# A decoder trunk on one core: key and content-query projections regrouped, mask and maximum in one operation, the keys' norm scale moved to the latents

## The chip, the cores and the metric

The kernel runs on one core of a Trainium2 chip. The metric is the device time of one execution in microseconds (us). A core has a matmul engine (TensorE, PE in the profile, with PEld for its weight loads), a vector engine (DVE), an activation engine (ACT), GpSimd (POOL) and SyncE (SP), which issues DMAs. Each engine takes its instructions in the order in which they stand in its queue, and waits on semaphores for the others.

## The reference

Two layers over 256 positions of width 2048. The first mixes by a short gated convolution, the second by latent attention with 16 heads; each is followed by a squared-ReLU MLP, and every sub-layer ends in a layer norm of (alpha * x + f(x)). What matters here is the attention:

```
ckv = h @ w_dkv
c = rms_norm(ckv[..., :512], kv_norm_g)
k_pe = apply_rope(ckv[..., 512:], cos, sin)
kv = (c @ w_ukv).reshape(bsz, seq, 16, 256)      # k_nope, v: 128 + 128 a head
...
q = (rms_norm(x @ w_dq, q_norm_g) @ w_uq).reshape(bsz, seq, 16, 192)   # q_nope 128, q_pe 64
...
s = (q_nope . k_nope + q_pe . k_pe) * 192 ** -0.5
s = where(k_pos <= q_pos, s, -inf)
p = softmax(s)
o = p . v,  then o @ w_o
```

The root-mean-square norm multiplies each position by one number, so it may be taken before the up-projection (on the latents `c`) or after it (on the keys and values).

## The kernel before

Everything is in float32, and the large products keep its precision by splitting both operands into a high part that the matmul's input format holds exactly and a low remainder. A product of split operands has three parts: high by high, low weight by high data, high weight by low data. Weights stream in as 128x1024 blocks (SP's queue), ACT casts the high part (`hi`, line 139), DVE subtracts it (`lo`, line 140), and PE multiplies. At most nine pairs of such parts are held (`WA`), so a cast waits for PE to be done with the pair nine places back.

The data operand of a product holds the high part in columns 0 to 255 and the low part in columns 256 to 511 of one tile. There are two ways to multiply with it:

- `mm` (line 283, by `mm_k1`, lines 279 to 281): three matmuls of 256 columns for each 128 rows of the inner dimension, all added into one 128x256 half of a PSUM bank.
- `high` and `low` (lines 261 and 265): one matmul of 512 columns, high weight by both halves of the data, and one of 256 columns, low weight by the high half. The result lies in two halves of the bank, which `whole` (lines 405 to 407) adds up: ACT copies one half to SBUF (tile `t`), DVE adds the other.

The attention stage begins with the latents. `latent` (line 992) is called four times for the key/value side (`chl`, 4 tiles) and four times for the queries (`qhl`): it finishes the layer norm of the product (`ln.weighted`), multiplies by the norm's gain and splits (lines 996 and 997), and sums squares (1000 to 1004). `rms` (1006) makes 1/rms per position, for the keys and values as a column `rc`; PE spreads it over the partitions and ACT copies it as the row tile `rk` (1043). The gain is on the latents; the position's scale is not: keys are multiplied by `rk` when they leave PSUM (line 1083, DVE), values by `rc` (line 1106, ACT). The queries' scale is folded into the exponent (`sc`, `nsc`).

`project` (line 1074) makes one group of four heads, four times: four keys `ps_k`, two tiles of rotary queries `ps_p`, four content queries `ps_q` (line 1095, ACT copies them out), two tiles of values `ps_v`. All of them, except the values, go through `mm`, in a ring of four PSUM banks. `attend` (1109) is one head: scores into `S`, mask added (1124, DVE, 128x384: the first block of queries sees 128 keys, the second 256), maximum of each of the two blocks (1126, DVE), exponent with its sum (1129, ACT), scaling (1131 to 1133, DVE), transposes, and the product with the values. `together` (1150) starts head s, transposes for head s-2 and finishes head s-3, and the loop puts three items of the next group's `project` behind each. A tile scheduler lays the instructions of each engine in a fixed order from this; lines of the code may so stand elsewhere in a queue than the text suggests. Between them DVE and ACT also do work without haste: the splits of later weights, and `normal` (529 to 531, tile `nu`), which finishes the layer norm of the residual.

Of the kernel before, what the change touches and what calls it, by code (L numbers as in the profile page):

```python
# [10 lines left out]
F32 = mybir.dt.float32  # L11
F32R = mybir.dt.float32r
AF = mybir.ActivationFunctionType
ALU = mybir.AluOpType
AX = mybir.AxisListType

P = 128
W = 256 + 2
T = 256
# [10 lines left out]
RMS_EPS = 1e-6  # L30
SCALE = (128 + 64) ** -0.5
NEG = -1e30
LOOK = 5
RAW, WA = 7, 9
NB = 4
# [21 lines left out]
def trunk(ctx: ExitStack, tc: tile.TileContext, xT, vecs, lead, w_first, w_in, w_out, w_kv, w_q, w_uk, w_uv,  # L57
# [201 lines left out]
    def high(ps, w, blk, x, first):  # L259

        nc.tensor.matmul(ps, w[blk // 8][0][:, blk % 8, :], x, start=first, stop=False)  # L261

    def low(ps, w, blk, x, last):

        nc.tensor.matmul(ps[:, :T], w[blk // 8][1][:, blk % 8, :], x[:, :T], start=False, stop=last)  # L265
# [17 lines left out]
    def mm(ps, w, b0, xhl, nk):  # L283

        for k in range(nk):
            mm_k1(ps, w, b0 + k, xhl[k], k == 0, k == nk - 1)
# [116 lines left out]
    def whole(ps, out):  # L403

        t = tmp.tile([P, T], F32, tag="evac", name="t")
        nc.scalar.copy(t, ps[:, T:])  # L406
        nc.vector.tensor_tensor(out, ps[:, :T], t, ALU.add)  # L407
# [560 lines left out]
    with tc.tile_pool(name="att", bufs=1) as ap:  # L968
# [13 lines left out]
        def rope(src):  # L982
# [6 lines left out]
            nc.vector.tensor_tensor(a, a, b, ALU.add)  # L989
            return a  # L990

        def latent(ps, m, dst, gcol, sqs):
            f = tmp.tile([P, T], F32, tag="fh", name="lat", bufs=3)
            ln.weighted(ps, f)
            g = vec[:, gcol + m:gcol + m + 1]
            nc.scalar.activation(dst[m][:, :T], f, AF.Copy, scale=g)
            nc.vector.scalar_tensor_tensor(dst[m][:, T:], f, g, dst[m][:, :T].bitcast(F32),
                                           ALU.mult, ALU.subtract)
            if m == 0:
                nc.scalar.activation(sqs, f, AF.Square)  # L1000
            else:
                sq = tmp.tile([P, T], F32, tag="sq", name="sq")
                nc.scalar.activation(sq, f, AF.Square)
                nc.vector.tensor_tensor(sqs, sqs, sq, ALU.add)
# [31 lines left out]
        for m in range(NK):  # L1036
            ps = next(pss)
            if m == 0:
                rms(rc, csq)
            if m == 2:  # L1040
                rkp = psum("rkp")
                spread(rkp, rc)
                nc.scalar.copy(rk, rkp[:, :T])
            latent(ps, m, qhl, C_QG, qsq)
        rq = small.tile([P, 2], F32, tag="rr", name="rq")

        def query_scale():
# [15 lines left out]
        with tc.tile_pool(name="att2", bufs=2) as a2, \  # L1063
# [10 lines left out]
            def project(g, box):  # L1074

                k4, q4, v4 = (t[g % 2] for t in (k2, q2, v2))
                p4 = [p2[(2 * g + j) % 3] for j in range(2)]
                box.update(k=k4, q=q4, p=p4, v=v4)
                w = take()
                for j in range(4):  # L1080
                    ps = psum("ps_k")
                    mm(ps, w, 4 * j, chl, NK)
                    nc.vector.tensor_tensor(k4[:, j, :], ps[:, :T], rk, ALU.mult)
                    yield
                w = take(1)
                for j in range(2):
                    ps = psum("ps_p")
                    mm(ps, w, 4 * j, qhl, NK)
                    stacked(p4[j], rope(ps[:, :T]))
                    yield  # L1090
                w = take()
                for j in range(4):
                    ps = psum("ps_q")
                    mm(ps, w, 4 * j, qhl, NK)
                    nc.scalar.copy(q4[:, j, :], ps[:, :T])
                    yield
                if g == 0:
                    query_scale()
                for _ in range(4):
                    ln.normal(next(todo))  # L1100
                w = take()
                for b in range(2):
                    ps = psum("ps_v")
                    for k in range(NK):
                        dot(ps, wide_rows(w[k // 2], k % 2), held(chl[k], b), k == 0, k == NK - 1)
                    nc.scalar.activation(v4[:, b, :], ps, AF.Copy, scale=rc[:, b:b + 1])
                    yield

            def attend(h, box):

                j = h % 4
                qn, kn = box["q"][:, j, :], box["k"][:, j, :]
                qp = box["p"][j // 2][:, j % 2, :]
                S = paux.tile([P, 512], F32, tag="S", name=f"S_{h}", bufs=2)
                spans = ((0, P), (P, T))
                for b, (at, n) in enumerate(spans):
                    tok = slice(b * P, (b + 1) * P)
                    nc.tensor.matmul(S[:, at:at + n], qn[:, tok], kn[:, :n], start=True, stop=False)
                    nc.tensor.matmul(S[:, at:at + n], qp[:, tok], kph[:, :n], start=False, stop=False)
                    nc.tensor.matmul(S[:, at:at + n], qp[:, tok], kpl[:, :n], start=False, stop=True)  # L1120
                pr = pr2[h % 2]
                mx = small.tile([P, 2], F32, tag="mx", name="mx")
                su = small.tile([P, 2], F32, tag="su", name="su")
                nc.vector.tensor_tensor(pr, S[:, :3 * P], mask_t, ALU.add)
                for b, (at, n) in enumerate(spans):
                    nc.vector.tensor_reduce(mx[:, b:b + 1], pr[:, at:at + n], AX.X, ALU.max)
                nc.vector.tensor_tensor(mx, mx, nsc, ALU.mult)
                for b, (at, n) in enumerate(spans):
                    nc.scalar.activation(pr[:, at:at + n], pr[:, at:at + n], AF.Exp, bias=mx[:, b:b + 1],
                                         scale=sc[:, b:b + 1], accum_out=su[:, b:b + 1])  # L1130
                nc.vector.reciprocal(su, su)
                for b, (at, n) in enumerate(spans):
                    nc.vector.tensor_scalar(pr[:, at:at + n], pr[:, at:at + n], su[:, b:b + 1], None, ALU.mult)
                yield
                tp = paux.tile([P, 512], F32, tag="ta", name="tp")
                for n in range(3):
                    nc.tensor.transpose(tp[:, n * P:(n + 1) * P], pr[:, n * P:(n + 1) * P], id_t)
                pt = pt2[h % 2]
                nc.scalar.copy(pt, tp[:, :3 * P])
                yield  # L1140
                po = paux.tile([P, 512], F32, tag="tb", name="po")
                vv = box["v"]
                nc.tensor.matmul(po[:, :T], vv[:, 0, j * P:(j + 1) * P], pt[:, :T], start=True, stop=False)
                nc.tensor.matmul(po[:, P:T], vv[:, 1, j * P:(j + 1) * P], pt[:, T:], start=False, stop=True)
                put_split(oT[h], po[:, :T])
                yield
# [261 lines left out]
```

## Time and profile before

| | us |
|---|---|
| median of 3 runs | 1988.34 (1988.27 to 1989.27) |
| the profiled execution | 1987.44 |
| its span (first to last instruction) | 1985.7 |
| the part from the first key product to the first output product alone | 1095.6 to 1227.0 |

A timeline row gives an instruction's start (us from the span's start), its duration, engine, line and tiles. Matmuls overlap: one of 256 columns is shown with 0.28 us, yet the next starts after 0.12. So PE's cost is read as the distance of starts. The same holds, less strongly, for DVE and ACT: a 128x256 DVE operation is shown with 0.42 us and the next starts 0.34 later.

### The profile page before, as it was taken

The numbers are of one execution on the slowest core, as the hardware profiler recorded it, in microseconds if no ns is written. First come the engines' busy times: TensorE is split into PE (matmuls) and PEld (weight loads), VectorE is DVE, ScalarE is ACT, GpSimd is POOL, SyncE is SP. The second block draws the span as 40 slices with busy tenths as digits, with TensorE's granted clock in tenths as the row PEclk, the third lists the DMA queues.
The fourth block names the chain that finished last, engine by engine and source line by source line (L and its number), as shares of the span: only waits on it lengthen the run. The fifth ranks groups of instructions, "written<-read, shape, count | busy, mean of one in ns | idle before, by whom it ended". The sixth has DMA issues, their size and how long they took to land.

```text
span 1985.7 us, 29654 instructions
## 1 busy us (share of the span) xinstructions
PE 1977.9 (100%) x11048; PEld 1727.4 (87%) x11048; DVE 1748.6 (88%) x2532; ACT 1285.2 (65%) x1902; POOL 36.0 (2%) x81
## 2 busy tenths in 40 slices
PE   9999999999999999999999999999999999999998
PEld 8888888988888888888889998898888888888886
DVE  8667667786999999999898988777799999999998
ACT  7444445585767767677666766557576776767765
POOL 0000000000000000000100110000000000000010
PEclk9999999999999999999999999999999999999999
DMA  9666666573666665666865644656355666556685
GB/s 343 213 190 189 188 188 190 179 237 134 194 210 203 203 208 192 212 203 202 271 236 175 198 125 141 206 182 195 115 198 202 207 206 207 191 203 211 202 245 179
DMA packets 111840, 395.77 MB, mean 199 GB/s; under 512 B 12752, under 2 KB 14800, under 8 KB 111184
## 3 DMA queue, kind: packets, MB, share of 16 engines
q1 hardware_dynamic: 106704, 383.79, 59.2%
q0 software_dynamic: 4848, 9.96, 2.2%
q8 instruction: 86, 1.41, 0.3%
q14 instruction: 58, 0.48, 0.1%
q10 hardware_dynamic: 144, 0.13, 0.0%
HBM read 384.40 MB, written 4.19 MB: 196 GB/s over the span
## 4 chain that ended last, share of the span: by engine, by line
PE 97%; DVE 1%; ACT 1%; issue 1%; DVEq 0%; ACTq 0%
PE ps_u L261 21%; PE ps_l L261 13%; PE ps_u L265 11%; PE ps L348 8%; PE ps L349 8%; PE ps L346 8%; PE ps_l L265 7%; PE ps_d L349 2%; PE ps_d L348 2%; PE ps_d L346 2%; PE ps_w L295 1%; PE ps_w L293 1%; PE ps_w L294 1%; PE ps_g L295 1%; PE ps_g L293 1%; PE ps_g L294 1%
## 5 line engine op out<-in xcount | busy, mean ns | idle before, releaser
L140 DVE TENSOR_TENSOR lo<-raw,hi 128x1024 fp32r<-128x1024 f32 x709 | 851.3, 1221 | 115.6 <-issue 46.9
L139 ACT CAST hi<-raw 128x1024 fp32r<-128x1024 f32 x709 | 726.8, 1049 | 329.4 <-DVE raw L182 134.3
L261 PE MATMUL ps_u<-xhl,hi 128*128 128x512 f32 x1792 | 621.0, 393 | 0.1
L265 PE MATMUL ps_u<-xhl,lo 128*128 128x256 f32 x1792 | 486.1, 280 | 0.0
L261 PEld LDWEIGHTS ps_u<-xhl,hi 128*128 128x128 f32 x1792 | 329.3, 188 | 66.5 <-DVE fp L407 0.5
L265 PEld LDWEIGHTS ps_u<-xhl,lo 128*128 128x128 f32 x1792 | 338.4, 189 | 12.8
L261 PE MATMUL ps_l<-xhl_a,hi 128*128 128x512 f32 x704 | 244.1, 393 | 0.0
L265 PE MATMUL ps_l<-xhl_a,lo 128*128 128x256 f32 x704 | 195.6, 280 | 0.0
L261 PEld LDWEIGHTS ps_l<-xhl_a,hi 128*128 128x128 f32 x704 | 132.3, 188 | 29.8
L265 PEld LDWEIGHTS ps_l<-xhl_a,lo 128*128 128x128 f32 x704 | 131.9, 188 | 0.2
L177 DVE TENSOR_TENSOR raw_t<-raw,raw 128x1024 f32<-128x1024 f32 x100 | 121.9, 1219 | 0.4 <-DMA raw<-in_w2f_dram 0.4
L140 DVE TENSOR_TENSOR lo_t<-raw_t,hi_t 128x1024 fp32r<-128x1024 f32 x100 | 121.9, 1219 | 0.0
L406 ACT COPY t<-ps_u 128x256 f32<-128x256 f32 x112 | 41.4, 369 | 108.6 <-PE ps_u L265 108.4
L139 ACT CAST hi_t<-raw_t 128x1024 fp32r<-128x1024 f32 x100 | 105.2, 1052 | 0.0
L261 PE MATMUL ps_l<-z,hi 128*128 128x512 f32 x240 | 82.4, 392 | 0.0
L295 PE MATMUL ps_w<-xd,hi 128*128 128x258 f32 x256 | 72.8, 284 | 0.0
L293 PE MATMUL ps_w<-xd,hi 128*128 128x258 f32 x256 | 72.3, 283 | 0.0
L407 DVE TENSOR_TENSOR fp<-ps_u,t 128x256 f32<-128x256 f32 x112 | 47.1, 420 | 28.7 <-ACT t L406 28.5
L294 PE MATMUL ps_w<-xd,lo 128*128 128x258 f32 x256 | 72.3, 282 | 0.0
L184 DVE TENSOR_TENSOR raw<-raw 128x512 f32<-128x512 f32 x100 | 69.2, 692 | 3.5
L261 PE MATMUL ps_l<-oT,hi 128*128 128x512 f32 x208 | 71.3, 392 | 0.0
L140 DVE TENSOR_TENSOR t<-raw,t 128x512 fp32r<-128x512 f32 x100 | 68.6, 686 | 2.1 <-ACT t L139 1.0
(378 smaller groups left out, 3921.2 us busy)
## 6 DMA issues: line engine op xcount, KB each, us to landing
raw<-in_w_dram SPq DMA_DIRECT2D x312, 512.0 KB, 4.2
raw<-in_w2f_dram SPq DMA_DIRECT2D x200, 512.0 KB, 4.2
raw<-in_w_in_dram SPq DMA_DIRECT2D x88, 512.0 KB, 4.3
raw<-in_w_out_dram SPq DMA_DIRECT2D x32, 512.0 KB, 4.2
raw<-in_w_o_dram SPq DMA_DIRECT2D x32, 512.0 KB, 4.3
raw<-in_w_kv_dram SPq DMA_DIRECT2D x10, 512.0 KB, 4.8
raw<-in_w_q_dram SPq DMA_DIRECT2D x8, 512.0 KB, 4.1
raw<-in_w_uk_dram SPq DMA_DIRECT2D x8, 512.0 KB, 4.3
```

The lines of the kernel that those rows point to most:

```text
L139: nc.scalar.copy(hi, src)
L140: return nc.vector.tensor_tensor(lo, src, hi.bitcast(F32), ALU.subtract)
L177: nc.vector.tensor_tensor(t.rearrange(two, a=2), b12.unsqueeze(1).to_broadcast([P, 2, BW]), r1.rearrange(two, a=2), ALU.subtract)
L184: nc.vector.tensor_tensor(t4, b21, b12, ALU.subtract)
L261: nc.tensor.matmul(ps, w[blk // 8][0][:, blk % 8, :], x, start=first, stop=False)
L265: nc.tensor.matmul(ps[:, :T], w[blk // 8][1][:, blk % 8, :], x[:, :T], start=False, stop=last)
L293: nc.tensor.matmul(ps[:, :W], hi, x[k][:, :W], start=k == 0, stop=False)
L294: nc.tensor.matmul(ps[:, :W], lo, x[k][:, :W], start=False, stop=False)
L295: nc.tensor.matmul(ps[:, :W], hi, x[k][:, W:], start=False, stop=k == NC - 1)
L346: nc.tensor.matmul(ps, x[0], w[0], start=first, stop=False, skip_group_check=onto)
L348: nc.tensor.matmul(ps[:, at], x[0], w[1][:, at], start=False, stop=False, skip_group_check=onto)
L349: nc.tensor.matmul(ps, x[1], w[0], start=False, stop=last, skip_group_check=onto)
```

## The change

Three edits.

1. Keys and content queries use `high` and `low`, a pair for each of the four inner blocks, in place of `mm`'s three matmuls, and `whole` in place of a single operation that takes the result out of PSUM. The rotary queries keep `mm`.
2. The keys' scale goes to the latents. `latent` leaves the four key/value latents unscaled in a tile `plain`; once `rk` is there, `normed` multiplies each by `rk` and splits it. It is called for tiles 0 and 1 behind the third query latent and for 2 and 3 behind the fourth. The products by `rk` and `rc` at keys and values go; values are copied.
3. Mask and maximum are one operation for each of the two blocks, `tensor_tensor_reduce`, which writes the masked scores and the maximum.

```
@@ -989,13 +990,22 @@
+        plain = act.tile([P, NK, T], F32, tag="a1", name="plain")
+
+        def gained(dst, f, g):
+            nc.scalar.activation(dst[:, :T], f, AF.Copy, scale=g)
+            nc.vector.scalar_tensor_tensor(dst[:, T:], f, g, dst[:, :T].bitcast(F32), ALU.mult, ALU.subtract)
+
+        def normed(m):
+            f = plain[:, m, :]
+            nc.vector.tensor_tensor(f, f, rk, ALU.mult)
+            gained(chl[m], f, vec[:, C_KG + m:C_KG + m + 1])
+
         def latent(ps, m, dst, gcol, sqs):
-            f = tmp.tile([P, T], F32, tag="fh", name="lat", bufs=3)
+            f = plain[:, m, :] if dst is chl else tmp.tile([P, T], F32, tag="fh", name="lat", bufs=3)
             ln.weighted(ps, f)
-            g = vec[:, gcol + m:gcol + m + 1]
-            nc.scalar.activation(dst[m][:, :T], f, AF.Copy, scale=g)
-            nc.vector.scalar_tensor_tensor(dst[m][:, T:], f, g, dst[m][:, :T].bitcast(F32),
-                                           ALU.mult, ALU.subtract)
+            if dst is not chl:
+                gained(dst[m], f, vec[:, gcol + m:gcol + m + 1])
...
             latent(ps, m, qhl, C_QG, qsq)
+            if m >= 2:
+                for k in range(2 * m - 4, 2 * m - 2):
+                    normed(k)
...
                     ps = psum("ps_k")
-                    mm(ps, w, 4 * j, chl, NK)
-                    nc.vector.tensor_tensor(k4[:, j, :], ps[:, :T], rk, ALU.mult)
+                    for k in range(NK):
+                        high(ps, w, 4 * j + k, chl[k], k == 0)
+                        low(ps, w, 4 * j + k, chl[k], k == NK - 1)
+                    whole(ps, k4[:, j, :])
...
                     ps = psum("ps_q")
-                    mm(ps, w, 4 * j, qhl, NK)
-                    nc.scalar.copy(q4[:, j, :], ps[:, :T])
+                    for k in range(NK):
+                        high(ps, w, 4 * j + k, qhl[k], k == 0)
+                        low(ps, w, 4 * j + k, qhl[k], k == NK - 1)
+                    whole(ps, q4[:, j, :])
...
-                    nc.scalar.activation(v4[:, b, :], ps, AF.Copy, scale=rc[:, b:b + 1])
+                    nc.scalar.copy(v4[:, b, :], ps)
...
-                nc.vector.tensor_tensor(pr, S[:, :3 * P], mask_t, ALU.add)
                 for b, (at, n) in enumerate(spans):
-                    nc.vector.tensor_reduce(mx[:, b:b + 1], pr[:, at:at + n], AX.X, ALU.max)
+                    nc.vector.tensor_tensor_reduce(pr[:, at:at + n], S[:, at:at + n], mask_t[:, at:at + n], 1.0, LOW,
+                                                   ALU.add, ALU.max, mx[:, b:b + 1])
```

The scheduler lays the queues anew for this. Three places follow. In the rows, a number behind a name is that of the buffer; `ps_w` is the product for a latent, `t` an intermediate, `lat` the tile that holds `chl` and `qhl`, `kqva1` the tile of the keys and queries, `kqva2` that of values, masked scores and mask. Lines from about 1000 on stand up to 17 lines later in the changed file, those before it one line later.

**TensorE, where the last query latent ends and the first key begins**, before:

```order
L293 MATMUL ps_w_10802<-xd1_0_9688,hi353_10655 128x258
L294 MATMUL ps_w_10802<-xd1_0_9688,lo353_10656 128x258
L295 MATMUL ps_w_10802<-xd1_0_9688,hi353_10655 128x258
L279 MATMUL ps_k_10904<-lat_10352,lo354_10662 128x256
L280 MATMUL ps_k_10904<-lat_10352,hi354_10661 128x256
L281 MATMUL ps_k_10904<-lat_10352,hi354_10661 128x256
```

and with the change:

```order
L294 MATMUL ps_w_10797<-xd1_0_9688,hi353_10644 128x258
L295 MATMUL ps_w_10797<-xd1_0_9688,lo353_10645 128x258
L296 MATMUL ps_w_10797<-xd1_0_9688,hi353_10644 128x258
L262 MATMUL ps_k_10905<-lat_10352,hi354_10650 128x512
L266 MATMUL ps_k_10905<-lat_10352,lo354_10651 128x256
```

The three matmuls of an inner block are two; nothing has come between the last latent and the first key.

**DVE, from the third query latent to the first keys**, before:

```order
L542 SCALAR_TENSOR_TENSOR t_10793<-ab1_10370,wgb_10791,t_10793 128x256
L140 TENSOR_TENSOR lo359_10895<-raw359_10892,hi359_10894 128x1024
L140 TENSOR_TENSOR lo360_10901<-raw360_10898,hi360_10900 128x1024
L997 SCALAR_TENSOR_TENSOR lat_10352<-lat_10790,vec_85,lat_10352 128x256
L1004 TENSOR_TENSOR squares_10363<-squares_10363,sq_10799 128x256
L140 TENSOR_TENSOR lo361_10963<-raw361_10960,hi361_10962 128x1024
L541 TENSOR_TENSOR t_10866<-ps_w_10802,ab1_10370 128x256
L140 TENSOR_TENSOR lo362_11021<-raw362_11018,hi362_11020 128x1024
L542 SCALAR_TENSOR_TENSOR t_10866<-ab1_10370,wgb_10864,t_10866 128x256
L1083 TENSOR_TENSOR kqva1_10878<-ps_k_10904,rk_10360 128x256
L1083 TENSOR_TENSOR kqva1_10878<-ps_k_10918,rk_10360 128x256
```

and with the change:

```order
L543 SCALAR_TENSOR_TENSOR t_10782<-ab1_10371,wgb_10780,t_10782 128x256
L1001 TENSOR_TENSOR plain_10363<-plain_10363,rk_10360 128x256 x4
L997 SCALAR_TENSOR_TENSOR lat_10352<-plain_10363,vec_85,lat_10352 128x256
L997 SCALAR_TENSOR_TENSOR lat_10352<-lat_10779,vec_85,lat_10352 128x256
L1014 TENSOR_TENSOR squares_10364<-squares_10364,sq_10788 128x256
L997 SCALAR_TENSOR_TENSOR lat_10352<-plain_10363,vec_85,lat_10352 128x256 x3
L141 TENSOR_TENSOR lo360_10902<-raw360_10899,hi360_10901 128x1024
L542 TENSOR_TENSOR t_10861<-ps_w_10797,ab1_10371 128x256
L141 TENSOR_TENSOR lo361_10956<-raw361_10953,hi361_10955 128x1024
L543 SCALAR_TENSOR_TENSOR t_10861<-ab1_10371,wgb_10859,t_10861 128x256
L408 TENSOR_TENSOR kqva1_10879<-ps_k_10905,t_10914 128x256
```

All eight operations of the four `normed` stand together, ahead of the last query latent (`ps_w_10797`) and of the splits 360 and 361; the split 359 has gone ahead of the first row shown.

**DVE in the second group of heads, round the scores of head 1 (`S_1`)**, before:

```order
L1127 TENSOR_TENSOR mx_11165<-mx_11165,nsc_10362 128x2
L1083 TENSOR_TENSOR kqva1_10878<-ps_k_11202,rk_10360 128x256
L530 TENSOR_TENSOR nu_11451<-nu_11451,ab1_10370 128x256
L529 TENSOR_TENSOR nu_11801<-xback_9683,ab1_10370 128x256
L140 TENSOR_TENSOR lo370_11352<-raw370_11349,hi370_11351 128x1024
L1083 TENSOR_TENSOR kqva1_10878<-ps_k_11216,rk_10360 128x256
L530 TENSOR_TENSOR nu_11801<-nu_11801,ab1_10370 128x256
L1124 TENSOR_TENSOR kqva2_10879<-S_1_11230,kqva2_10879 128x384
L529 TENSOR_TENSOR nu_11805<-xback_9683,ab1_10370 128x256
L1131 RECIPROCAL su_11166<-su_11166 128x2
```

and with the change:

```order
L1142 ISA kqva2_10880,mx_11215<-S_1_11208,kqva2_10880 128x256
L1142 ISA mx_11215 128x1
L1148 RECIPROCAL su_11151<-su_11151 128x2
L530 TENSOR_TENSOR nu_11412<-xback_9683,ab1_10371 128x256
L1150 TENSOR_SCALAR kqva2_10880<-kqva2_10880,su_11151 128x128
L1150 TENSOR_SCALAR kqva2_10880<-kqva2_10880,su_11151 128x256
L408 TENSOR_TENSOR kqva1_10879<-ps_k_11184,t_11193 128x256
L408 TENSOR_TENSOR kqva1_10879<-ps_k_11196,t_11205 128x256
L1144 TENSOR_TENSOR mx_11215<-mx_11215,nsc_10362 128x2
```

The fused operation (`ISA`; the rows show that of the second block, that of the first stands just ahead) is two instructions, the second of which writes the maximum alone. The second and third keys of the group (`ps_k_11184`, `ps_k_11196`) were taken out of PSUM ahead of head 0's reciprocal (`su_11166`); now they stand behind it (`su_11151`) and behind the scaling of head 0.

1 line of the change is left out of this document (added).

## The prediction

> **What bounds the kernel now.** First the page's busy shares, its clock row, and the shares of the chain that ended last, by engine; then the waits of TensorE over the whole span.
>
> ```profile
> span 1985.7 us, 29654 instructions
> PE 1977.9 (100%) x11048; PEld 1727.4 (87%) x11048; DVE 1748.6 (88%) x2532; ACT 1285.2 (65%) x1902; POOL 36.0 (2%) x81
> PEclk9999999999999999999999999999999999999999
> PE 97%; DVE 1%; ACT 1%; issue 1%; DVEq 0%; ACTq 0%
> ...
> PE po L1143 <- DVE oT L412: 0.2, 1, 0.2
> ```
>
> TensorE is busy throughout at full clock, it is 97% of the chain, and the last row is the only wait listed for it in the attention stage, 0.2 us. So time is won only by giving TensorE less to do, and lost only by making it wait. The change touches the attention stage. The busy time by stretches of its heads, in the order PE, PEld, DVE, ACT, POOL, shows who could become late:
>
> ```profile
> 1095.00:1113.00 18.00, 18.00 (x143) 17.55 (x142) 17.51 (x39) 12.00 (x22) 2.91 (x6) 1.00 0.64 210
> 1113.00:1150.00 37.00, 37.00 (x266) 35.08 (x265) 34.94 (x93) 29.23 (x59) 4.92 (x11) 1.00 0.60 180
> 1150.00:1185.00 35.00, 35.00 (x260) 33.52 (x260) 27.34 (x67) 20.90 (x48) 4.00 (x8) 1.00 0.42 129
> 1185.00:1215.00 30.00, 29.75 (x191) 26.83 (x191) 25.82 (x70) 17.29 (x46) 3.96 (x8) 1.00 0.39 115
> ```
>
> DVE has 0.49 us free in the first stretch, 2.06 in the second, 7.66 and 4.18 in the others: 14.4 of 120. ACT has 40.6. The change gives both more work, so DVE in the first two stretches is the place to watch.
>
> **Term 1, the matmuls.** The four keys of the first group start at 1095.62 and the rotary queries follow at 1101.37; a pair as the change uses it runs in the output projection.
>
> ```profile
> 1095.62 0.28 PE L279 MATMUL ps_k<-lat,lo 128*128 128x256 f32 x1
> 1101.37 0.28 PE L279 MATMUL ps_p<-lat,lo 128*128 128x256 f32 x1
> ...
> 1239.72 0.39 PE L261 MATMUL ps_l<-oT,hi 128*128 128x512 f32 x1
> 1245.96 0.39 PE L261 MATMUL ps_l<-oT,hi 128*128 128x512 f32 x1
> L281 PE MATMUL ps_k<-lat,hi x64: 278/283/288, 1095.9 to 1179.6; 128*128 128x256 f32 x64
> L281 PE MATMUL ps_q<-lat,hi x64: 278/283/288, 1104.5 to 1192.4; 128*128 128x256 f32 x64
> ```
>
> The first distance holds 16 triples (four keys by four inner blocks): 5.75 / 16 = 0.359 us each. The second holds 18 pairs: 6.24 / 18 = 0.347. Line 281 runs once a triple, 64 times for keys and 64 for queries, so 128 triples become pairs: 128 x 0.0127 = **-1.6 us**. All of it is on the path, since TensorE doesn't wait here. The columns streamed are the same, 768; what goes is one instruction's fixed cost in each block.
>
> By the Trainium skill, VectorE: DVE Perf Modes, in its cycle table by engine, a matmul takes 6 cycles and its columns at 2.4 GHz. That would make one instruction less worth 2.5 ns, and term 1 only -0.3 us; the trace's rows, at 12.7 ns, disagree with it for these products, and the sum goes by the rows.
>
> **Term 2, the statistics of the keys.** TensorE waits before the first `rstat`:
>
> ```profile
> 1079.46 0.48 DVE L997 SCALAR_TENSOR_TENSOR lat<-lat,vec 128x256 fp32r<-128x256 f32 x1
> 1079.86 0.42 DVE L1004 TENSOR_TENSOR squares<-squares,sq 128x256 f32<-128x256 f32 x1
> 1079.99 0.28 PE L294 MATMUL ps_w<-xd,lo 128*128 128x258 f32 x1
> 1080.19 0.42 DVE L541 TENSOR_TENSOR t<-ps_w,ab 128x256 f32<-128x256 f32 x1
> 1080.33 0.61 PE L1010 MATMUL rstat<-col,squares 128*128 128x1 f32 x4
> ```
>
> The step is 0.34 where 0.12 is usual, so 0.22 is a wait for the sum of squares, which ends at 1080.28. With the change four splits of 0.40 between starts (`lat`, line 997) go from DVE's queue ahead of that sum, so it may end 1.6 earlier. `rstat` stands nine matmuls earlier on TensorE, 9 x 0.12 = 1.1. Since 1.6 is over 1.1 + 0.22, I take the wait as gone: **-0.2 us**; were DVE to move up less, 0.
>
> **Term 3, are the scaled latents there when the first key starts?** Before, `chl` was long done; now it is made last. DVE's rows of before at this place, and when `rk` is there:
>
> ```profile
> 1090.84 0.37 ACT L1043 COPY rk<-rkp 128x256 f32<-128x256 f32 x1
> ...
> 1092.37 0.48 DVE L542 SCALAR_TENSOR_TENSOR t<-ab,wgb,t 128x256 f32<-128x256 f32 x1
> 1092.76 2.36 DVE L140 TENSOR_TENSOR lo<-raw,hi 128x1024 fp32r<-128x1024 f32 x2
> 1095.04 0.48 DVE L997 SCALAR_TENSOR_TENSOR lat<-lat,vec 128x256 fp32r<-128x256 f32 x1
> ```
>
> By starts, a weight split costs 2.28 / 2 = 1.14, and from term 2's rows a 128x256 split 0.40, a sum 0.33. In the changed order there stand behind the row of 1092.37: four products by `rk`, five such splits (one of them the query's) and one sum: 5 x 0.33 + 5 x 0.40 = 3.65. If the queue stands no later at that row than before, it is done with them at 1092.76 + 3.65 = 1096.41, and the last result lands some 0.1 later. The first key needs tile 3 three pairs behind its start, at 1095.62 + 3 x 0.35 - 0.2 = 1096.46, tiles 0 to 2 before that; these are made 0.4 apart, as TensorE asks for them 0.35 apart. ACT makes the high parts beside it; it has 6.0 us free in the first stretch alone. So they meet within a tenth or two. The two weight splits pushed back (360, 361) belong to the first group's last items and to the second group. I take **+0.1 us**, with 0 to 1.5 for the range: 1.14 is what one more weight split ahead of them would cost.
>
> **Term 4, results out of PSUM.** Keys: a product on DVE becomes a copy on ACT and a sum on DVE of the same size. Queries: the copy on ACT stays, a DVE sum of 0.33 comes in, 16 of them: 5.3 us of DVE. ACT has 16 copies more; at the 0.37 of such a copy (row of 1090.84), 5.9 us against 40.6 free. The bank of a key is used again four items later. The narrowest place is the second group: the second key's sum now stands behind the scaling of head 0, which waits for the first exponent and its table load.
>
> ```profile
> 1121.20 1.28 ACT L1129 ACT_TABLE_LOAD   x1
> 1123.48 0.19 ACT L1129 ACTIVATION_READ_ACCUMULATOR kqva<-kqva,mx,sc 128x1 f32 x1
> 1123.91 0.28 PE L279 MATMUL ps_p<-lat,lo 128*128 128x256 f32 x1
> 1124.07 0.16 DVE L1131 RECIPROCAL su<-su 128x2 f32<-128x2 f32 x1
> 1124.33 0.55 DVE L1133 TENSOR_SCALAR kqva<-kqva,su 128x128 f32<-128x128 f32 x2
> 1126.79 0.49 PE L1137 MATMUL tp<-id_t,kqva 128*128 128x128 f32 x3
> ```
>
> That key's bank goes to the group's second `ps_p`, 12 x 0.12 = 1.44 behind the first: 1125.35 in before. By then 48 pairs and terms 2 and 3 have put TensorE ahead by 0.7, so it asks at 1124.65. The cast ahead of the table load waits for keys on TensorE and moves with it; from the end of the exponent's sum, 1123.67 less 0.6, come the reciprocal, a `nu`, two scalings and the key's sum, 0.16 + 0.33 + 0.55 + 0.42 = 1.5: 1124.55. Cover of 0.1 only; **+0.1**, 0 to 1. In the third and fourth group no table is loaded and DVE has 7.66 and 4.18 us free.
>
> **Term 5, mask and maximum.** The operation isn't in the trace. What it replaces:
>
> ```profile
> 1117.95 0.55 DVE L1124 TENSOR_TENSOR kqva<-S,kqva 128x384 f32<-128x384 f32 x1
> 1118.42 1.22 DVE L140 TENSOR_TENSOR lo<-raw,hi 128x1024 fp32r<-128x1024 f32 x1
> 1119.55 0.61 DVE L1126 TENSOR_REDUCE mx<-kqva 128x1 f32<-128x128 f32 x2
> 1120.07 0.42 DVE L1083 TENSOR_TENSOR kqva<-ps_k,rk 128x256 f32<-128x256 f32 x1
> L513 DVE RECIPROCAL iv<-var x3: 1746/1746/1753, 385.2 to 1322.3; 128x256 f32<-128x256 f32 x3
> ```
>
> That is 0.47 + 0.52 = 0.99 a head. From below: two sums of 128 and 256 columns without a price for the maximum, 0.19 + 0.33 = 0.52 (384 and 256 columns cost 0.47 and 0.33, so 128 cost 0.19). From above, however far: DVE's slowest operation for its size, the reciprocal, 1.75 x 384 / 256 = 2.6. I take the nearest row, the sum, and for the two reads of one column the whole 0.16 of the small reciprocal (row of 1124.07): 0.84, which gives back 0.15 x 16 = 2.4 us of the 5.3 above. None of it is on TensorE's path while DVE keeps up: **0**.
>
> By the Trainium skill, VectorE: DVE Perf Modes, Rules for kernel authors, fusing on this engine is not worth it for its own sake, because every operation drains the pipe: fewer operations count. The fused form is four instructions for three, so by that rule it would gain nothing; by the rows a small one costs 0.16 at most, and the sum of three is 0.99 against 0.84. With either, DVE's balance changes and the sum doesn't.
>
> **Term 6, the rest.** Values by a copy in place of a scaled copy, and the scale's product moved: beside other work on ACT and DVE, 0.
>
> **The sum** is -1.6 - 0.2 + 0.1 + 0.1 = -1.6 us. The profiled execution took 1987.44 (the span and 1.74 around it), so it would take 1985.8; the median of the runs shown, 1988.34, is 0.9 above it, and gives **1986.7**.
>
> **Rivals.** *A wait takes the place of the matmul saved:* the first key waits for the latents, or the ring of banks for the sums. For it: the covers are 0.1 us or less, and DVE is 97% busy from 1095 to 1113. Against it: the scheduler has put the four `normed` ahead of the splits. One or two weight splits late cost 1.1 to 2.3 us in place of 0.2: 1987.6 to 1988.8, no change.
>
> *DVE becomes the bound, slower:* the fused operation costs more than its parts. Up to 1150 DVE has 2.55 us free, 8 sums (2.6) come in and four heads' masks go; head 0's scaling is done at 1124.88 and transposed at 1126.79, 1.9 us of cover. So it decides from 0.99 + 2 / 4, about 1.5 us a head. At 2.0 it loses 4 - 2 = 2 by 1150 and 12 - (11.84 - 2.6) = 2.8 later, 4.8 - 1.6 = +3.2: 1991.5. At 2.6, 4.4 + 10.1 - 1.6 = +12.9: 2001. Against it: no row has a two-operand operation at that price.
>
> *The change doesn't shorten the matmuls:* if the pair cost 0.359, the sum is 0: 1988.3. Against it: the 18 pairs above, on the same engine at the same clock.
>
> *More than the sum:* terms 3 and 4 at 0 and the listed wait of 0.2 gone too: 1986.3; beyond that no row offers anything.
>
> **How the numbers follow.** The forecast (1985.2 to 1987.4) 0.62; the new wait 0.18; DVE the bound 0.11; no saving 0.06; something below 1985.2 0.03. The likeliest gives 1986.7. The range takes in the new wait and the start of the bound by DVE, to 1990.0, and leaves out about 0.12 in all. A measurement of this kernel tells 0.2% from no change, 4 us: so faster (below 1984.4) 0.03, slower (above 1992.3) 0.07, within it 0.90.
>
> **What would show it.** Sixteen pairs of the first keys in 5.55 us, not 5.75; no step over 0.2 us between the last `ps_w` and the fourth pair, nor before the second group's `ps_p`; the `rstat` step back to usual; the fused operation with its read at 0.3 to 0.5 us; DVE's busy time from 1095 to 1215 within 2 us of 105.6. It would be wrong if TensorE showed waits for `lat` or for the sum at line 408, or if the fused operation took over 0.7 us a block.

## The result, and the profile after

The changed kernel takes 1985.58 us, the median of 21 runs (1984.65 to 1986.40), against 1988.34 for the kernel before (21 runs beside them, 1987.35 to 1990.25). The ratio is 0.9986, with a 95% interval of 0.9979 to 0.9992: 1.6 to 4.2 us less. The gain is clear of the noise and small: 0.14%, inside the 0.2% that the prediction counts as no change. The forecast was 1986.7. The profiled execution took 1985.18, against 1987.44 before, 2.26 less; what follows is read from these two executions.

The page of the changed kernel, its busy shares, its clock row and the chain by engine:

```profile
span 1983.4 us, 29464 instructions
PE 1976.0 (100%) x10920; PEld 1719.8 (87%) x10920; DVE 1747.5 (88%) x2568; ACT 1290.7 (65%) x1918; POOL 35.9 (2%) x81
PEclk9999999999999999999999999999999999999999
PE 98%; DVE 1%; ACT 1%; issue 0%; DVEq 0%
```

TensorE has 128 instructions fewer (11048 to 10920), as counted from the diff, and is still the chain. Its whole list of waits, where before there stood a third row, `po` for `oT`:

```profile
PE ps L1275 <- issue: 1.5, 1, 1.5
PE warm L424 <- DVE col L425: 1.1, 1, 1.1
```

The busy time by the four stretches, in the order PE, PEld, DVE, ACT, POOL:

```profile
1095.00:1113.00 18.00, 18.00 (x111) 15.98 (x110) 17.81 (x42) 13.98 (x27) 3.25 (x7) 1.00 0.45 132
1113.00:1150.00 37.00, 37.00 (x226) 33.18 (x225) 36.74 (x103) 30.46 (x66) 4.58 (x10) 1.00 0.61 195
1150.00:1185.00 35.00, 35.00 (x224) 31.80 (x224) 29.02 (x83) 24.14 (x55) 3.90 (x8) 1.00 0.43 129
1185.00:1215.00 30.00, 30.00 (x181) 26.68 (x180) 23.39 (x80) 19.14 (x47) 3.90 (x8) 1.00 0.39 115
```

DVE's sum is 106.96 (105.60 before). Up to 1150 it has 0.45 us free of 55, and TensorE's column is full all the same: with this order of its queue a full DVE is not a late one.

**Where the 2.26 us are.** TensorE doesn't stop, so the distance between two of its rows that both kernels have is the price of what lies between. Two such rows enclose the changed stage: the last `lnAB` of the layer norm, and the first `ps_l` of the projection behind the attention. Before:

```profile
1061.70 0.40 PE L502 MATMUL lnAB<-sq,ones 128*128 128x512 f32 x1
1227.00 0.40 PE L261 MATMUL ps_l<-oT,hi 128*128 128x512 f32 x1
```

and after, with the starts of the first group's parts between them:

```profile
1061.64 0.40 PE L503 MATMUL lnAB<-sq,ones 128*128 128x512 f32 x1
1078.85 0.28 PE L295 MATMUL ps_w<-xd,lo 128*128 128x258 f32 x1
1078.97 0.50 PE L1020 MATMUL rstat<-col,squares 128*128 128x1 f32 x4
...
1095.28 0.40 PE L262 MATMUL ps_k<-lat,hi 128*128 128x512 f32 x1
1100.83 0.28 PE L280 MATMUL ps_p<-lat,lo 128*128 128x256 f32 x1
1103.69 0.40 PE L262 MATMUL ps_q<-lat,hi 128*128 128x512 f32 x1
1109.35 0.50 PE L1020 MATMUL rstat<-col,squares 128*128 128x1 f32 x4
...
1224.78 0.40 PE L262 MATMUL ps_l<-oT,hi 128*128 128x512 f32 x1
```

The stage went from 165.30 to 163.14, so 2.16 of the 2.26 lie in it. The reader sees the first `rstat` 0.12 behind the matmul ahead of it, where it was 0.34; 16 pairs of the keys in 5.55; and 16 of the queries in 5.66. The same subtraction, part by part, over the whole stage:

| part of TensorE's order | before | after | gain |
|---|---|---|---|
| statistics and latents (`ps_w`, `rstat`) | | | 0.28 |
| keys, four groups | 5.75 + 3 x 4.32 + 3 x 1.42 | 5.55 + 3 x 4.17 + 1.39 + 1.41 + 1.40 | 0.71 |
| queries, four groups | 5.76 + 3 x 4.32 + 3 x 1.43 | 5.66 + 4.17 + 2 x 4.24 + 3 x 1.40 | 0.49 |
| two steps of `ps_wo` and the `po` behind each, in the last heads | 1.56 + 0.73 and 2.36 + 0.73 | 1.22 + 0.65 and 2.12 + 0.65 | 0.74 |
| the rest | | | -0.06 |

The fourth line wasn't in the prediction. Here is what stood there before, TensorE, ACT and DVE in order of time; `po` is the product of one head's probabilities and values, and its bank is free when DVE has made the low part of `oT` (line 412):

```profile
1195.82 0.49 ACT L1129 ACTIVATE kqva<-kqva,mx,sc 128x128 f32<-128x128 f32 x1 [1.61 <-DVE mx L1127]
1200.20 1.04 ACT L139 CAST hi<-raw 128x1024 fp32r<-128x1024 f32 x1
1201.27 1.23 DVE L140 TENSOR_TENSOR lo<-raw,hi 128x1024 fp32r<-128x1024 f32 x1 [0.30 <-ACT hi L139]
1202.41 0.42 DVE L412 TENSOR_TENSOR oT<-po,oT 128x256 fp32r<-128x256 f32 x1
1202.54 0.27 PE L265 MATMUL ps_wo<-oT,lo 128*128 128x256 f32 x1
1202.98 0.67 PE L1143 MATMUL po<-kqva 128*128 128x256 f32 x2 [0.16 <-DVE oT L412]
```

TensorE asked at 1202.54 + 0.12 = 1202.66 and started at 1202.98: 0.32, where the list of waits puts 0.2. On DVE `oT` stood behind a weight split that waited for its cast; on ACT that cast stood behind two others and behind the exponent, which had waited 1.61 for the mask's maximum. After, the same place:

```profile
1192.49 0.49 ACT L1146 ACTIVATE kqva<-kqva,mx,sc 128x128 f32<-128x128 f32 x1 [0.37 <-DVE mx L1144]
1197.13 1.05 ACT L140 CAST hi<-raw 128x1024 fp32r<-128x1024 f32 x1
1198.21 1.23 DVE L141 TENSOR_TENSOR lo<-raw,hi 128x1024 fp32r<-128x1024 f32 x1 [0.61 <-ACT hi L140]
1199.35 0.42 DVE L413 TENSOR_TENSOR oT<-po,oT 128x256 fp32r<-128x256 f32 x1
1200.96 0.27 PE L266 MATMUL ps_wo<-oT,lo 128*128 128x256 f32 x1
1201.07 0.59 PE L1160 MATMUL po<-kqva 128*128 128x256 f32 x2
```

`oT` ends 1.30 ahead of `po`; before, TensorE had waited for it. The second of the two steps (2.36) ends in a wait of 0.25 that the list doesn't show: `po` was due at 1211.33 + 0.12 = 1211.45 and started at 1211.70. There `oT` ran on DVE from 1211.14 to 1211.56, behind a head's scaling and work of the next layer norm, with no weight split ahead of it.

### The profile page after: what moved, and what is told of

The parts are those of the page before. It is cut to its first block, busy times and chain, and to the rows that moved or that the text cites. A ratio compares the mean times of both kernels' runs of the same rounds, so it can differ in the third digit from the quotient of the medians.

```text
span 1983.4 us, 29464 instructions
## 1 busy us (share of the span) xinstructions
PE 1976.0 (100%) x10920; PEld 1719.8 (87%) x10920; DVE 1747.5 (88%) x2568; ACT 1290.7 (65%) x1918; POOL 35.9 (2%) x81
## 3 DMA queue, kind: packets, MB, share of 16 engines
q8 instruction: 85, 1.39, 0.3%
## 4 chain that ended last, share of the span: by engine, by line
PE 98%; DVE 1%; ACT 1%; issue 0%; DVEq 0%
PE ps_u L262 21%; PE ps_l L262 13%; PE ps_u L266 11%; PE ps L349 8%; PE ps L350 8%; PE ps L347 8%; PE ps_l L266 7%; PE ps_d L349 2%; PE ps_d L347 2%; PE ps_d L350 2%; PE ps_w L296 2%; PE ps_w L295 2%; PE ps_w L294 2%; PE ps_g L296 1%; PE ps_g L294 1%; PE ps_g L295 1%
```

## The experiments

Theory A: the gain is the matmuls, the statistics, and a new order on DVE's queue that puts a weight split of the last heads elsewhere. Theory B: the waits of the last heads went because the fused mask is shorter. The first four runs do one part of the change alone, or all of it but one. The stage is read from one profiled execution of each run; by time, none of the first three can be told from the kernel before, since their intervals take in 1. (The weight splits have numbers in the program's order; 388 to 390 are those of the last heads.)

**Queries by pairs alone** (the kernel before, with)

```
-                    mm(ps, w, 4 * j, qhl, NK)
-                    nc.scalar.copy(q4[:, j, :], ps[:, :T])
+                    for k in range(NK):
+                        high(ps, w, 4 * j + k, qhl[k], k == 0)
+                        low(ps, w, 4 * j + k, qhl[k], k == NK - 1)
+                    whole(ps, q4[:, j, :])
```

> The kernel before with the content queries alone by pairs of matmuls and the two-step way out of PSUM. The stage is counted from the second statistics matmul (lnAB) to the first output product alone (ps_l): 165.30 us before, 163.14 with the whole change. Theory A (matmuls plus the order of DVE's queue): 64 triples fewer give 0.5 to 0.8; the first wait of the tail (0.42 at 1202.6 in the kernel before, a product with the values that waits for DVE behind three weight splits) is gone, since the split 388 stands ahead of head 11's scaling here as in the changed kernel; the wait for the keys' statistics (0.27) stays: stage 164.1 to 164.4. Theory B (the fused mask shortens the chain of the softmax and so takes the tail's waits away): the tail's waits stay, 164.5 to 164.8.

Measured: 1987.10, ratio 0.9995 (0.9986 to 1.0003). The stage takes 164.17: 0.51 of its gain of 1.13 are in the queries' own steps, the rest in the last heads.

**Fused mask alone** (the kernel before, with)

```
-                nc.vector.tensor_tensor(pr, S[:, :3 * P], mask_t, ALU.add)
                 for b, (at, n) in enumerate(spans):
-                    nc.vector.tensor_reduce(mx[:, b:b + 1], pr[:, at:at + n], AX.X, ALU.max)
+                    nc.vector.tensor_tensor_reduce(pr[:, at:at + n], S[:, at:at + n], mask_t[:, at:at + n], 1.0, LOW,
+                                                   ALU.add, ALU.max, mx[:, b:b + 1])
```

> The kernel before with mask and maximum in one operation and nothing else. Theory A: the first wait of the tail stays, since three weight splits stand between head 11's scaling and the evacuation, as before; stage 164.9 to 165.3 (the second wait of the tail, 0.32 at 1211.5, may go, since less DVE work stands ahead of it). Theory B: both waits of the tail go, 164.6. If the fused operation costs more than its parts: over 165.3.

Measured: 1987.61, ratio 0.9999 (0.9990 to 1.0008). The stage takes 164.65, a gain of 0.65, all of it in the last heads.

**Scale on the latents alone** (the changed kernel with keys and queries by triples, and the mask as before)

```
-                    for k in range(NK):
-                        high(ps, w, 4 * j + k, chl[k], k == 0)
-                        low(ps, w, 4 * j + k, chl[k], k == NK - 1)
-                    whole(ps, k4[:, j, :])
+                    mm(ps, w, 4 * j, chl, NK)
+                    nc.vector.tensor_copy(k4[:, j, :], ps[:, :T])
```

> The keys' scale on the latents alone: keys by three matmuls, copied out by DVE; queries, mask and maximum as before. Theory A: the wait for the keys' statistics (0.27) goes, nothing else: stage 165.0, both waits of the tail as before. Rival: the scaled latents come late and the first key waits, more than 0.2 us between the last latent's product and the fourth inner block: 165.5 or more.

Measured: 1987.38, ratio 0.9997 (0.9988 to 1.0006). The stage takes 164.39: 0.28 in the statistics, some 0.63 in the last heads.

**All but the mask** (the changed kernel with the mask's lines of before)

> The changed kernel with mask and maximum in three operations as before. Theory A: the pairs (1.3), the statistics' wait (0.27) and the first wait of the tail (0.42) go all the same: stage 163.1 to 163.5. Theory B: the tail's waits are back, 163.8 or more. The fused operation's share of the time is the difference to the changed kernel, 0 to 0.35.

Measured: 1985.79, ratio 0.9988 (0.9979 to 0.9997); the stage takes 163.18, against 163.14 with the fused mask. Beside the rest of the change the fused operation is worth 0.04 us in these two profiles, and by time it can't be told from nothing (1985.79 against 1985.58).

So the 0.6 of the last heads came with each of three parts alone, and once with all. Neither theory says that. The mask is as before in three of the four runs, so a shorter mask isn't needed. With the fused mask alone and with the scale alone, DVE does three weight splits between a head's scaling and `oT`, in the order of before, and `oT` ends 1.0 and 0.7 us ahead of its `po` all the same; so the place of the split isn't needed either. Two readings were left: the chain of the last heads is a few tenths short in the kernel before, and any part that frees a little mends it; or the one profiled execution of before waited there by accident.

**The kernel before, once more**, unchanged.

> The kernel before, unchanged, profiled once more. In its first profile the stage from the last layer-norm weights to the first output projection took 165.30 us, and TensorE took 1.56 and 2.36 us for the two output-product steps at the end of the heads, where every changed kernel so far took 1.2 and 2.1. Chain theory (the last heads' chain of mask, exponent, copies, splits and transposes is 0.4 us short of what TensorE asks, always): 165.2 to 165.4 again, with steps of 1.5 to 1.6 and 2.3 to 2.4. Fluke theory (that one execution waited there, others do not): 164.6 to 164.8, with steps of 1.2 and 2.1; then the gain of 0.6 found in the changed kernels isn't theirs.

Measured: 1988.05 in the profiled execution, the stage 165.64. From its waits:

```profile
PE po L1143 <- DVE oT L412: 0.5, 1, 0.5
```

The steps are 1.88 and 2.38. The second is as expected; the first and the stage lie outside their windows, on the side away from an accident. The waits belong to the kernel before, and the size of the first differs between executions, by 0.3 in these two.

**The fused mask alone, twice a head.** In the fused loop of the second run,

```
-                for b, (at, n) in enumerate(spans):
+                for b, (at, n) in 2 * tuple(enumerate(spans)):
```

> The kernel before with the fused mask and maximum alone, done twice a head with the same result. Once (the single edit) it took both waits at the end of the heads away: stage 164.65, steps 1.2 and 2.1. Chain theory: the mask step of a head is then 1.34 long by DVE's starts, where before it was 0.99 to 1.23, so the last heads' chain is again as late as before or later: the waits are back, stage 165.2 to 166.2, steps of 1.5 to 2.1 and 2.3 to 2.7. Rival, that it was the new place of the instructions and not the chain's length: 164.65 again.

Measured: 1987.47, the stage 164.65, steps of 1.23 and 2.12. The chain theory, as put, misses: the operations are longer and no wait comes back. Its timeline on DVE tells why the test didn't do what it was for:

```profile
1192.38 0.28 DVE L1126 CUSTOM_DVE_ANT_0 kqva<-S,kqva 128x128 f32<-128x128 f32 x1
...
1193.60 0.16 DVE L1128 TENSOR_TENSOR mx<-mx,nsc 128x2 f32<-128x2 f32 x1
...
1200.43 1.23 DVE L141 TENSOR_TENSOR lo<-raw,hi 128x1024 fp32r<-128x1024 f32 x1 [0.70 <-ACT hi L140]
1201.58 0.42 DVE L413 TENSOR_TENSOR oT<-po,oT 128x256 fp32r<-128x256 f32 x1
```

The head's maximum is there at 1193.60, where in the kernel before it was made at 1195.56, although that kernel is 0.55 ahead on TensorE at this place. The scheduler has put the mask forward among the weight splits, and `oT` ends 1.20 ahead of its `po`. So an edit here changes lengths and order at once. What is shown: both waits are those of `po` for an `oT` that comes late on DVE, the first behind weight splits; they are there in both profiles of before, and no profile of a kernel with any part of the change has them. What brings `oT` forward in each of these kernels, shorter work or a new order further ahead on the queues, was not separated.

**A matmul of 512 columns cut into two**, to measure one instruction by itself; line 262 and its call outside the attention:

```
-            high(ps, w, k, x[k], k == 0)
+            weight = w[k // 8][0][:, k % 8, :]
+            for at in (slice(0, T), slice(T, 2 * T)):
+                nc.tensor.matmul(ps[:, at], weight, x[k][:, at], start=k == 0 and at.start == 0, stop=False)
```

> The changed kernel with 1792 of its 512-column matmuls, outside the attention stage, each cut into two of 256 columns: the same columns streamed, 1792 instructions more and nothing else, on an engine that is busy throughout. By the prediction's rows (12.7 ns for one instruction) +22.8 us: 2008. By what the keys showed (11 ns) +20: 2005.5; by the queries (7.7 ns) +13.8: 1999. By 2.5 ns, worked out from the Trainium skill's VectorE: DVE Perf Modes, cycle table by engine (6 cycles at 2.4 GHz), +4.5: 1990.

Measured: 2006.33, with this row on its page:

```profile
PE 1997.1 (100%) x12728; PEld 1817.5 (91%) x12728; DVE 1749.2 (87%) x2568; ACT 1291.6 (64%) x1918; POOL 35.9 (2%) x81
```

12728 - 10920 = 1808 instructions more (the loop also runs 16 that the expectation hadn't counted), and 2006.33 - 1985.18 = 21.15 us, from one execution of each kernel: 11.7 ns each, between the keys' 11 and the prediction's 12.7. Each of them brings a weight load too (PEld counts the same 1808 more), so this is the price of a matmul and its load together. What share the load has was not measured. It may have one: in the stretch from 1095 to 1113 PEld was busy for 17.55 of 18.00 us before the change and for 15.98 after.

**The mask twice and three times in the changed kernel**, by the same edit of its loop, with 2 and with 3. (Where other work follows at once, a mask more costs 0.55 us by the starts of DVE's rows, and not the 0.67 that both expectations take: there the next operation needs the read's result and starts 0.12 later.)

> The changed kernel with the fused mask and maximum done twice a head, with the same result: DVE gets 16 x 0.67 = 10.7 us more between 1095 and 1215, a head's mask then costs 1.34. By the prediction's threshold (DVE decides from about 1.5 us a head) nothing is lost in the first stretches: the stage 163.1 to 163.6. Rival, DVE or the chain of the last heads is at its bound already: +0.4 or more from the two waits at the end of the heads, which come back, and +1 or more if the second group waits as well: 164.1 or more.

Measured: 1985.53, ratio 0.9987 (0.9978 to 0.9996); the stage takes 163.14, as with the mask done once.

> The changed kernel with the fused operation three times a head, same result: 2.01 us of DVE a head, 21.4 us more in all. By the prediction's rival (DVE is the bound from 1.5 us a head; at 2.0 a loss of 2.0 up to 1150 us and 2.8 later) the stage takes 163.14 + 4.8 = 168, the kernel 1990. By DVE's free time alone (13.0 us of 120 free in the changed kernel) 21.4 - 13.0 = +8.4: 1993.6. Rival, the weight splits are far enough ahead that the work finds room beyond the heads: 163.2 to 164.2, 1985.2 to 1986.2.

Measured: 1986.10, ratio 0.9988 (0.9977 to 0.9997); the stage takes 163.74, so two more masks in every head cost 0.6 in all. Its last three stretches, and behind them the one that follows (the first has 17.81 on DVE, as after the change):

```profile
1113.00:1150.00 37.00, 37.00 (x227) 33.17 (x226) 35.97 (x127) 27.31 (x59) 4.30 (x9) 1.00 0.55 175
1150.00:1185.00 35.00, 35.00 (x225) 31.79 (x224) 34.60 (x132) 25.29 (x58) 4.63 (x10) 1.00 0.41 135
1185.00:1215.00 30.00, 29.82 (x178) 26.31 (x177) 29.62 (x123) 20.21 (x49) 3.19 (x7) 1.00 0.45 133
1215.00:1250.00 35.00, 35.00 (x203) 30.68 (x203) 31.27 (x65) 20.78 (x36) 0.00 (x0) 1.00 0.56 186
```

DVE is busy 118.0 of the 120 us, 11.0 more than after the change, and 3.4 more in the stretch behind (31.27 against 27.85). The mask's work found room because other work of DVE moved back. In the second stretch the masks went from 3.19 to 8.91 us, and yet DVE's busy time fell from 36.74 to 35.97. What moved is mostly work without haste: of the 11 `nu` products and 11 `nu` sums of `normal` that DVE did in that stretch, 4 and 4 are left, and 10 of 15 products of the next layer norm (`xback`) went behind 1215. The weight splits hardly moved: 32 start from 1095 to 1215 in both, one fewer in the second and in the third stretch and two more in the fourth. TensorE first shows a gap in the third row, 29.82 of 30.00, at a matmul of the next layer norm (`mu0p`).

**The scaled latents split twice**, to push them onto the path:

```
-            gained(chl[m], f, vec[:, C_KG + m:C_KG + m + 1])
+            for _ in range(2):
+                gained(chl[m], f, vec[:, C_KG + m:C_KG + m + 1])
```

> The changed kernel with the scaled key latents split twice, same result: eight operations of 0.40 us on DVE in place of four, and on its queue the last tile's two now stand behind one weight split. From the rows of the changed kernel the last result would land at about 99.2 us where TensorE wants it at 96.3: if the making of the latents stands on the path of the first key (term 3), it loses 2.9 us there, at once and for good: the first group's keys in 8.4 us in place of 5.55, the stage 166.0, the kernel 1988. Rival: the loss is made up later in the stage, since the splits run ahead: 163.2 to 164.

Measured: 1990.83, the stage 168.27, so 5.1 more than after the change. Neither theory gives that. Its waits:

```profile
PE ps_p L280 <- DVE kqva L408: 2.4, 1, 2.4
...
PE ps_k L262 <- DVE lat L997: 0.2, 1, 0.2
```

At the first keys it loses 0.9 and not 2.9, since TensorE's order was changed too: it multiplies the first two tiles for all four keys, eight pairs, before it asks for the third (at 1098.84) and the fourth. The larger loss came at the place of term 4, the second group's second `ps_p`. DVE and TensorE there:

```profile
1123.45 2.35 DVE L141 TENSOR_TENSOR lo<-raw,hi 128x1024 fp32r<-128x1024 f32 x2
...
1127.00 0.55 DVE L1151 TENSOR_SCALAR kqva<-kqva,su 128x128 f32<-128x128 f32 x2
1127.46 0.75 DVE L408 TENSOR_TENSOR kqva<-ps_k,t 128x256 f32<-128x256 f32 x2
1127.94 0.39 PE L280 MATMUL ps_p<-lat,lo 128*128 128x256 f32 x1 [2.38 <-DVE kqva L408]
```

Two weight splits in one go, then head 0's scaling, then the key's sum that frees the bank. With 1.6 us more of DVE's work ahead of the first key, and the queues laid anew for it, TensorE lost 3.2 at this `ps_p` and 1.0 right behind it. What share the work has in that, and what share the new order, was not separated.

**Rotary queries by pairs too**, in all groups, and in all but the first, to see whether term 1 can be had once more:

```
-                    mm(ps, w, 4 * j, qhl, NK)
-                    stacked(p4[j], rope(ps[:, :T]))
+                    for k in range(NK):
+                        high(ps, w, 4 * j + k, qhl[k], k == 0)
+                        low(ps, w, 4 * j + k, qhl[k], k == NK - 1)
+                    f = tmp.tile([P, T], F32, tag="fh", name="fq", bufs=3)
+                    whole(ps, f)
+                    stacked(p4[j], rope(f))
```

> The changed kernel with the rotary queries by pairs of 512 and 256 columns too, 32 triples fewer, each result then put together in SBUF by one more copy on ACT and one sum on DVE before its rotation. Theory that only the instruction's price counts: 32 x 0.011 = -0.35, the stage 162.8 us against 163.14, the kernel 1985.2. Rival: the copy and the sum make the rotated queries late, or hold the bank, and TensorE waits: 163.1 or more.

Measured: 1985.79, ratio 0.9987 (0.9978 to 0.9996). The rotary steps gain 0.28, but the stage takes 163.35, 0.21 more than the changed kernel's. Most of the loss stands in the first group, where the query's sum of squares is late:

```profile
PE rstat L1020 <- DVE kqva L408: 0.2, 1, 0.2
```

> The changed kernel with the rotary queries by pairs in all groups but the first, 24 triples fewer. With all four groups the pairs won 0.29 in their own steps and lost 0.5 in the first group, where DVE has 0.2 us free of 18: the sum of squares and the first scores came late. Theory: without the first group nothing waits, the stage takes 163.14 - 0.2 = 162.95, the kernel 1985.0, the fastest of all by a little. Rival: there too a wait takes the gain's place: 163.1 or more.

Measured: 1985.49, ratio 0.9986 (0.9977 to 0.9995). The stage takes 162.96, 0.18 less than the changed kernel's, and nothing waits in it. It is the shortest stage of all; by time the kernel can't be told from the changed one (1985.58), and its profiled execution, 1986.92, was 1.9 us longer outside the stage.

## Why the prediction was right, and where its sum was off

The signs that it named came: 16 pairs in 5.55, no wait at the two places, the `rstat` step at 0.12, the fused operation with its read at 0.36 and 0.50, DVE within 2 us of its sum.

**What bounds the kernel** holds: TensorE is 98% of the chain, and a DVE with 0.45 us free of 55 didn't make it wait.

**Term 1** had the right mechanism and was sized too large: -1.6 forecast, -0.71 - 0.49 = -1.2 measured. A key's pair gains 0.71 / 64 = 11 ns, a query's 7.7, not 12.7. The long runs of keys met the forecast (5.75 to 5.55 for 16, 4.32 to 4.17 for 12: 12.5 ns a pair). The four pairs of a group's last key, which stand alone between scores and rotary queries, gained 0.07 / 12 = 6 ns. Of the queries' long runs only the second group's gained 12.5 ns, the others 6 to 7 (5.76 to 5.66, 4.32 to 4.24). Their 512-column matmul lasts longer, by the groups of the page's fifth part with the shapes kept apart (busy us, then mean ns):

```profile
L262 PE MATMUL ps_q<-lat,hi 128*128 128x512 f32 x64 | 22.9, 397 | 0.0
L262 PE MATMUL ps_k<-lat,hi 128*128 128x512 f32 x64 | 22.6, 393 | 0.0
```

Same shape, same clock, 4 ns apart; what makes them differ was not found. The rule of the Trainium skill weighed at this term (VectorE: DVE Perf Modes, the cycle table by engine), an estimate of 2.5 ns for a matmul more from its 6 cycles at 2.4 GHz, does not price it here: the run that adds 1808 of them, each with its weight load, took 11.7 ns for each. That the whole of it is a fixed cost of the instruction, as the prediction says, is not shown; the load may hold a part.

**Term 2** was right: the wait of 0.22 went, and `rstat` itself took 0.11 less, 0.28 net of small differences. The run with the scale alone has the same 0.28, and the two without it have none, so the scale on the latents is the cause.

**Terms 3 and 4** were forecast at +0.1 each and cost nothing. DVE's rows at the first key, after:

```profile
1092.00 1.43 DVE L1001 TENSOR_TENSOR plain<-plain,rk 128x256 f32<-128x256 f32 x4
...
1094.46 1.27 DVE L997 SCALAR_TENSOR_TENSOR lat<-plain,vec,lat 128x256 fp32r<-128x256 f32 x3
...
1123.22 0.54 DVE L1150 TENSOR_SCALAR kqva<-kqva,su 128x128 f32<-128x128 f32 x2
1123.68 0.75 DVE L408 TENSOR_TENSOR kqva<-ps_k,t 128x256 f32<-128x256 f32 x2
```

The last latent is done at 1095.73, where TensorE wants it at 1095.28 + 3 x 0.35 = 1096.3: 0.6 to spare, as the queue stood 0.76 earlier at that point than the working assumed (1092.00, not 1092.76). In the second group the sum of the second key, the first of the two in the last row, ends at about 1124.1, and the second `ps_p` starts at 1123.05 + 1.43 = 1124.48: 0.4 to spare, where 0.1 was reckoned. These were the right places to watch: the run that splits the latents twice lost 0.9 at the one and 3.2 at the other.

**Term 5.** Nothing on the path, as forecast. The price lay between the lower bound of 0.52 and the 0.84 taken:

```profile
L1142 DVE CUSTOM_DVE_ANT_0 kqva<-S,kqva x32: 278/352/426, 1117.4 to 1212.1; 128x128 f32<-128x128 f32 x16, 128x256 f32<-128x256 f32 x16
L1142 DVE DVE_READ_ACCUMULATOR2_ANT mx<- x32: 77/83/90, 1117.6 to 1212.4; 128x1 f32 x32
```

By starts (1191.62, 1191.83, 1192.17 in DVE's rows, and 1192.29 for what follows) a head costs 0.67, against 0.84 taken and 0.99 before: 5.1 us given back for the 5.3 of new sums. On the page of the fused mask alone DVE is 6.6 us less busy than before (1742.0 against 1748.6). The second rule of the Trainium skill that was weighed (VectorE: DVE Perf Modes, Rules for kernel authors: fewer operations count, fusing by itself isn't worth it) didn't hold for DVE's time, since four instructions cost a third less than three, 0.67 against 0.99 us; for the kernel's time it came to the same, 0.04 us.

**What the sum missed** is the fourth line of the table. The prediction held the listed wait of 0.2 for all that the last heads offered, in its rival "more than the sum" ("beyond that no row offers anything"). The listed idle time is only part of such a wait: the steps before and behind it were longer by 0.74 in that profile, 0.6 net of two later steps that got longer. With -1.2 - 0.3 - 0.6 the sum is -2.1, the 2.16 of the stage, and 1985.58 lies between the forecast's 1986.7 and its lower end. That term 1 fell short by 0.4 while 0.6 came that was not forecast is luck: the two nearly cancel. Of the 1.1 us between forecast and measurement the sum makes about 0.6. The rest comes from the starting point: the profiled execution of before lies 0.9 below its median, that of after 0.4. One cause is seen: in the second profile of before the first wait of the last heads is 0.3 longer.

**The rivals.** The new wait didn't come. That DVE is the bound from 1.5 us a head was tried at about 1.7, since three masks cost some 1.7 by starts and not 2.0. The reckoning (four heads at 0.7 more than before, less the 2 us of cover) then gives a loss of 0.8 before 1150 and none behind it; measured, nothing was lost before 1150, and 0.6 in the last heads. The step that failed is to take DVE's busy time in a stretch as a fixed load: `nu` and a few other operations moved to later stretches. What a head at 2.0 or more would cost stays open.

## What to carry to other kernels

Where one engine never stops, compare its steps row by row between two profiles: the list of waits had 0.2 us where the steps showed 0.6. Gains of single edits don't add when each of them ends the same small wait: three parts alone gained 1.13, 0.65 and 0.91 of the stage, and 0.6 of that was the same in all three. Work added to an engine that has hardly any free time can cost nothing (a second mask in each of 16 heads, 0.55 us apiece: none) or three times itself (1.6 us ahead of the first key: 5.1). In these two runs it turned on whether the scheduler left it ahead of something that TensorE asks for next, and on how much of the work beside it could wait.

## What the runs showed of the hardware

A matmul instruction more, with its weight load and with the same columns streamed, costs 11.7 ns at full clock (1808 of them, 21.15 us). The fused sum and maximum takes 278 to 426 ns for blocks of 128 and 256 columns, and the read of its result 0.08 us.
